# Softplus moved into attention, another product order in the MLPs' last quarter, and new orders of casts and scans

## The chip, the core and the metric

The kernel runs on one core of a Trainium2 chip. The metric is the device time of one execution in microseconds (us); of several runs the median is given. A core has five engines with queues of their own, which run each in order: TensorE (PE: matmuls and transposes), VectorE (DVE), ScalarE (ACT: activations, copies and casts), GpSimd (POOL) and SyncE (SP), which mainly issues DMA transfers. They wait for each other by semaphores.

## The reference, cut to what matters

Two layers over 512 tokens of width 1024, all in float32. Layer 0 mixes by stick-breaking attention with 16 heads, layer 1 by a gated linear recurrence (RG-LRU); each is followed by an MLP with squared ReLU.

```python
def stick_breaking_attention(h, w_qkv, w_o):      # per block of 128 queries
    z = einsum(q, k) * scale
    log_keep = where(mask, log_sigmoid(-z), 0)
    after = reversed_cumsum(log_keep) - log_keep
    w = where(mask, exp(log_sigmoid(z) + after), 0)
    return (w @ v) @ w_o

def rglru_block(h, w_in, ...):
    gate = gelu((h @ w_in)[..., :W])
    xc = causal_depthwise_conv((h @ w_in)[..., W:], conv_w, conv_b)     # 4 taps
    r = sigmoid(xc @ w_a + b_a);  i = sigmoid(xc @ w_x + b_x)           # 16 diagonal blocks
    log_a = -8 * r * softplus(-lam)
    a = exp(log_a);  b = sqrt(-expm1(2 * log_a)) * (i * xc)
    hs = associative_scan(a, b)                                         # h = a h + b
    return (hs * gate) @ w_o

def squared_relu_mlp(h, w1, w2):
    u = relu(h @ w1)
    return (u * u) @ w2

for layer in range(2):
    x = x + mixer(rms_norm(x, norm_mix[layer]))
    x = x + squared_relu_mlp(rms_norm(x, norm_mlp[layer]), w1, w2)
return rms_norm(x, norm_final)
```

## The kernel before

**Products.** Activations lie transposed, features on 128 partitions and 512 tokens in the free dimension, in eight chunks (`C` = 8). Every float32 product is done as three matmuls on operands split in two: a weight slab of 128x1024 is loaded by SP into `raw`, ScalarE casts it to `wh` (high part) and VectorE subtracts to give `wl` (low part) (`slab`, L184 and L191; for the MLP's second matrix `operand`, L834 and L835); the activations are split in the same way (`xgh`/`xgl` at L115 and L116, or `bh`/`bl`). `three` (L196 to L198) then issues high by high, high by low, low by high.

**Order.** The order on TensorE is the order in which the program emits its matmuls; a scheduler sets the order on the other engines, from the same emission order, and `tc.issue_after(i)` and `tc.high_priority()` bend it: with the first, what stands inside goes on its own engine behind instruction `i`. As each engine works its queue in order, a cast placed behind another instruction also waits for whatever that one waits for.

**Start.** The first slabs of q and k are loaded and cast in parts (`slab_parts`), x arrives in eight chunks, each cast by L115. `softplus` is a generator that computes `c4` and `c8` from the RG-LRU's lambda: absolute value, a sigmoid (L232), then 24 small VectorE operations on 128x8 tiles with a polynomial (L234 to L246). The first `yield` stands behind the sigmoid; its second piece is emitted in mid attention (`next(soft)`), its parts go where the scheduler finds place, which is from 8.6 us on. What it makes is first needed by `recur` in the RG-LRU. ScalarE's functions lie in tables; changing from one table to another appears in the trace as an ACT_TABLE_LOAD.

**Attention.** Eight pairs of heads. `score_steps(pair)` computes scores (L525, L526), two sigmoids on ScalarE (`w` at L533, `keep` at L534), a scan on VectorE (L542) and a product on GpSimd (L546). `value_steps(pair)` takes eight turns, one per head of the pair and block of keys: `turn` transposes the weights on TensorE (L564), ScalarE casts the head (`th`, L579), VectorE subtracts the tail (`tl`, L580), and `times` multiplies by the values (L590, L591). Between those steps `fill` puts matmuls that don't depend on them: projections of the next pair's q and k (`qk_steps`), of values (`v_steps`, L441 to L443), and, at the end, parts of the output product (`so_part`, `so_steps`, L196 to L198 on `bh`). Each `fill` step that starts a new weight begins with its `slab`: the DMA, the casts and the subtractions are emitted right there. Steps of scores and values are due at fixed counts of fill steps.

**MLP.** The second product of each MLP is done in four quarters (`q4`), each as seven block products P1 to P7 in place of eight (`PRODUCTS`); the weights' blocks are summed on VectorE (L854) or, for the names in `far`, by an accumulating DMA of GpSimd, then cast and cut (`operand`). A product has two groups `g`; `block` prepares its weight, `times` issues its matmuls (L866), `collect` adds its result to `c` (L875). In the last quarter the sums wait behind `self.ready`, the last split of activations (L815).

**RG-LRU.** For each of eight chunks: `conv` (projection, taps at L1058, cast to `bh`/`bl` at L1064 and L1065), `gates` (two gate products, L1078 to L1080, and sigmoids), `recur` (Tanh L1096, Exp L1098, Sqrt L1104 on ScalarE, the scan on VectorE), `gate` and `gated`. A list at the end of the stage gives their order.

**Tail.** `square` takes sums of squares of the finished rows (L1177), `finish` the bias (L1189), the root (L1190) and the scaling. For the last rows, two halves' sums are added first (L1225).

Of the kernel before, what the change touches and what calls it, by code (L numbers as in the profile page):

```python
# [47 lines left out]
def hybrid_encoder(  # L48
# [123 lines left out]
    adding, behind = [False], [None]  # L172

    def slab(src, cut=1, ks=range(C)):
# [7 lines left out]
        for i in range(cut):  # L182
            k = slice(ks.start + i * len(ks) // cut, ks.start + (i + 1) * len(ks) // cut)
            A.copy(wh[:, k, :], raw[:, k, :])  # L184
# [41 lines left out]
    def softplus():  # L226

        ab, pp, den, s1, s2, pl, _, _ = lams.values()
        lam = col("lam")
        V.tensor_scalar(ab, lam, -1.0, None, ALU.mult)  # L230
        V.tensor_tensor(ab, ab, lam, ALU.max)
        A.activation(pp, ab, AF.Sigmoid, scale=-1.0)  # L232
        yield
        V.tensor_scalar(den, pp, -1.0, 2.0, ALU.mult, ALU.add)  # L234
# [14 lines left out]
    soft = softplus()  # L249

# [12 lines left out]
    with ExitStack() as actx:  # L263
# [250 lines left out]
        late = {}  # L514
        turns = [0]

        def score_steps(pair):

            for j in range(2):
                for qb in range(NB):  # L520
# [13 lines left out]
                    A.activation(keep[:, :n], z[:, :n], AF.Sigmoid, scale=norm["rn"][:, qb : qb + 1])  # L534
# [21 lines left out]
        def value_steps(pair):  # L556
# [3 lines left out]
            def turn(j, kb):  # L560
# [17 lines left out]
                with tc.high_priority():  # L578
                    A.copy(dh, tr[:, :n])  # L579
                    left[j, kb] = V.tensor_tensor(dl, tr[:, :n], f(dh), ALU.subtract)  # L580

# [28 lines left out]
            for g in order[-2:]:  # L610
                times(*g)
                yield
            A.copy(bh[:, pair, :], o)
# [45 lines left out]
        for i in range(n_fill):  # L659
# [14 lines left out]
            if i == LATE // 2:  # L674

                next(soft)
# [42 lines left out]
    class Mlp:  # L719
# [109 lines left out]
        def operand(self, raw):  # L829
# [5 lines left out]
            V.tensor_tensor(wl, raw, f(wh), ALU.subtract)  # L835
            return wh, wl

        def block(self, q4, name, g, far):
# [11 lines left out]
            elif to:  # L850

                ahead = not far or (name, g) == ("P5", 0)
                with nullcontext() if ahead else tc.issue_after(self.ready.ins):
                    V.tensor_tensor(raw, raw, self.raws[to, g], ALU.add)  # L854
# [25 lines left out]
        def down(self, q4, far=(), end=None):  # L880
            sums = {}

            def product(name, g):
                w = self.block(q4, name, g, far)
# [6 lines left out]
                if g:  # L891
                    for i in range(2):
                        self.collect(name, i, sums[to][i])
# [7 lines left out]
            for g in range(2):  # L901
                for name in ("P1", "P5", "P2"):
                    product(name, g)
            for name in ("P6", "P3", "P7"):
                for g in range(2):
                    product(name, g)
            end([self.block(q4, "P4", g, far) for g in range(2)], sums["X"])
# [28 lines left out]
    with ExitStack() as mctx:  # L936
# [25 lines left out]
        def between(q4, c):  # L962
            if (q4, c) == (0, C - 1):
                next(soft)
# [27 lines left out]
    with ExitStack() as rctx:  # L992
# [29 lines left out]
        xc, aa, om, z, hs, gin, gw = ({} for _ in range(7))  # L1022
# [66 lines left out]
        def recur(chunks):  # L1089
            nonlocal mark  # L1090

            for c in chunks:
                a0 = rp2.tile([P, S], F32, tag="a0", name="a0")
                d = rp2.tile([P, S], F32, tag="d", name="d")
                with after(sig):
                    ex = A.activation(om[c], aa[c], AF.Tanh, scale=c4[:, c : c + 1])  # L1096
                with after(ex):
                    ex = A.activation(a0, aa[c], AF.Exp, scale=c8[:, c : c + 1])  # L1098
                V.scalar_tensor_tensor(d, a0, 1.0, om[c], ALU.add, ALU.mult)
                G.tensor_scalar(aa[c], d, -1.0, 1.0, ALU.mult, ALU.add)  # L1100
                V.scalar_tensor_tensor(xc[c], a0, 1.0, xc[c], ALU.add, ALU.mult)
            for c in chunks:
                with after(ex):
# [3 lines left out]
                with after(tap if c < 6 else None):  # L1107
# [18 lines left out]
        for what, c in (  # L1126
            (conv, 0), (conv, 1), (conv, 2), (gate, 0), (gate, 1), (gates, 0), (conv, 3), (gates, 1),
            (gate, 2), (gates, 2), (conv, 4), (gates, 3), (recur, range(3)), (conv, 5), (gates, 4),
            (gate, 3), (conv, 6), (gates, 5), (gate, 4), (conv, 7), (recur, range(3, 6)), (gates, 6),
            (gate, 5), (gated, range(6)), (gate, 6), (gates, 7), (recur, range(6, C)), (gate, 7),  # L1130
# [21 lines left out]
    with ExitStack() as mctx:  # L1152
# [22 lines left out]
        def square(t, h, i, cols=slice(0, S)):  # L1175
# [3 lines left out]
            )  # L1179

# [4 lines left out]
        def finish(t, h, i, cut=None):  # L1185
# [3 lines left out]
            V.tensor_scalar(bias[:, t : t + 1], ss[:, t, 0:1], 1.0 / D, EPS, ALU.mult, ALU.add)  # L1189
# [12 lines left out]
        def end(ws, xs):  # L1202
            for t in range(2):
                square(t, 0, 0)
                scaled(t, 0)
                square(t, 1, 1)
# [7 lines left out]
            square(2, 0, 1)  # L1214
# [80 lines left out]
```

## Time and profile before

| | |
|---|---|
| median of 3 runs | 1083.8 us (1083.19 to 1087.09) |
| profiled execution | 1083.88 us |
| its span, first to last instruction | 1081.9 us |
| mean granted TensorE clock | 0.996 |
| busy: PE, DVE, ACT, POOL | 1061.7, 823.7, 569.5, 171.3 us |
| HBM read, written | 104.91 MB, 2.10 MB |

The profile is of one execution. A row of its timeline gives the start in us from the span's start, the duration in us, engine, line and operation, the tile written and those read, the shape, and in brackets how long the engine was idle before it and whom it waited for. Successive matmuls overlap, so their distance in time is from start to start. The granted clock is the share of full speed that the throttle gave TensorE.

### The profile page before, as it was taken

The page shows a single profiled execution, that of the slowest core. Times are in us where ns is not written, and L with a number is a line of the kernel's source. Part 1 is how long each engine was busy: PE and PEld are TensorE (multiplying, and loading weights), DVE is VectorE, ACT ScalarE, POOL GpSimd, SP SyncE. Part 2 cuts the span into 40 slices and gives each one's busy share as a digit, 9 for nine tenths or more (in the row PEclk, how much of TensorE's full clock was granted, in tenths as well). Part 3 has the DMA queues.
Part 4 walks back from the last instruction along what each step waited for, and adds up shares of the span by engine and source line. Part 5 has one row for each costly group of instructions (what it writes and reads, how often), then busy time and mean ns, then how long its engine had stood idle before and what let it go on. Part 6 is the DMA issues. An engine that isn't in the chain of part 4 may idle for free.

```text
span 1081.9 us, 13604 instructions
## 1 busy us (share of the span) xinstructions
PE 1061.7 (98%) x4992; PEld 880.2 (81%) x4992; DVE 823.7 (76%) x1078; ACT 569.5 (53%) x823; POOL 171.3 (16%) x199
## 2 busy tenths in 40 slices
PE   8999999999999999999999999999999999999987
PEld 7888888888888888888878777887888888888876
DVE  7788787838796597597687769975686597597686
ACT  7667676726455344344345468853454344344344
POOL 2344344420000000000001564122000000000002
PEclk8999999999999999999999999999999999999999
DMA  6754454426305305305332695252305305305103
GB/s 211 200 137 137 100 157 105 140 96 235 105 9 186 117 3 192 117 1 185 100 84 61 166 217 140 78 175 98 98 23 191 98 20 181 111 20 177 57 13 104
DMA packets 44034, 125.71 MB, mean 116 GB/s; under 512 B 7744, under 2 KB 8512, under 8 KB 43968
## 3 DMA queue, kind: packets, MB, share of 16 engines
q1 hardware_dynamic: 41088, 115.94, 34.4%
q0 software_dynamic: 2304, 8.39, 4.5%
q8 instruction: 39, 0.64, 0.3%
q10 hardware_dynamic: 576, 0.52, 0.1%
q14 instruction: 27, 0.22, 0.1%
HBM read 104.91 MB, written 2.10 MB: 99 GB/s over the span
## 4 chain that ended last, share of the span: by engine, by line
PE 84%; DVE 6%; ACT 5%; DMA 3%; issue 1%; SPq 0%; ACTq 0%; DVEq 0%
PE ps_t L866 10%; PE ps_o L866 6%; PE ps_acc L196 6%; PE ps_acc L197 6%; PE ps_acc L198 6%; PE ps_z L866 6%; PE ps_acc L866 5%; PE ps_o L196 4%; PE ps_o L198 4%; PE ps_o L197 4%; PE ps_t L197 3%; PE ps_t L196 3%; PE ps_t L198 3%; PE ps_z L196 3%; PE ps_z L197 3%; PE ps_z L198 3%
## 5 line engine op out<-in xcount | busy, mean ns | idle before, releaser
L184 ACT CAST wh<-raw 128x1024 fp32r<-128x1024 f32 (+2 forms) x136 | 119.8, 901 | 132.7 <-PE ps_o L198 33.4
L834 ACT CAST wh<-b 128x1024 fp32r<-128x1024 f32 x96 | 100.6, 1051 | 134.1 <-PE ps_o L866 25.0
L191 DVE TENSOR_TENSOR wl<-raw,wh 128x1024 fp32r<-128x1024 f32 (+2 forms) x126 | 131.7, 1062 | 24.9 <-ACT wh L184 24.8
L835 DVE TENSOR_TENSOR wl<-b,wh 128x1024 fp32r<-128x1024 f32 x96 | 117.5, 1226 | 27.0 <-ACT wh L834 26.9
L196 PE MATMUL ps_acc<-xgh,wh 128*128 128x512 f32 x304 | 123.7, 407 | 2.1 <-ACT xgh L115 1.4
L197 PE MATMUL ps_acc<-xgh,wl 128*128 128x512 f32 x304 | 120.2, 395 | 0.3 <-DVE wl L166 0.3
L198 PE MATMUL ps_acc<-xgl,wh 128*128 128x512 f32 x304 | 119.9, 395 | 0.0
L849 POOL DMA_DIRECT2D b<-in_w_dn x6 | 5.4, 903 | 639.6 <-DVE wl L835 316.9
L542 DVE TENSOR_TENSOR_SCAN scan<-keep,later 128x128 f32<-128x128 f32 (+1 forms) x64 | 60.6, 948 | 18.7 <-ACT keep L534 10.3
L196 PE MATMUL ps_o<-xgh,wh 128*128 128x512 f32 x176 | 69.5, 395 | 0.2 <-DVE x L695 0.2
L197 PE MATMUL ps_o<-xgh,wl 128*128 128x512 f32 x176 | 68.6, 390 | 0.0
L198 PE MATMUL ps_o<-xgl,wh 128*128 128x512 f32 x176 | 68.6, 390 | 0.0
L198 PEld LDWEIGHTS ps_acc<-xgl,wh 128*128 128x128 f32 x304 | 57.7, 190 | 12.9 <-DVE xgl L116 0.3
L196 PEld LDWEIGHTS ps_acc<-xgh,wh 128*128 128x128 f32 x304 | 57.8, 190 | 12.8 <-ACT xgh L115 1.8
L788 ACT ACTIVATE u<-u 128x512 f32<-128x512 f32 x64 | 39.3, 629 | 52.5 <-DVE u L787 52.5
L196 PE MATMUL ps_t<-xgh,wh 128*128 128x512 f32 x168 | 66.5, 396 | 0.0
L197 PEld LDWEIGHTS ps_acc<-xgh,wl 128*128 128x128 f32 x304 | 58.0, 191 | 10.2 <-DVE wl L166 0.6
L197 PE MATMUL ps_t<-xgh,wl 128*128 128x512 f32 x168 | 65.7, 391 | 0.0
L198 PE MATMUL ps_t<-xgl,wh 128*128 128x512 f32 x168 | 65.5, 390 | 0.0
L546 POOL TENSOR_TENSOR w<-w,scan 128x128 f32<-128x128 f32 (+1 forms) x64 | 53.4, 836 | 52.4 <-DVE scan L542 49.7
L854 DVE TENSOR_TENSOR b<-b,b 128x1024 f32<-128x1024 f32 x46 | 55.7, 1219 | 0.2
L798 DVE TENSOR_TENSOR u<-u 128x256 f32<-128x256 f32 x128 | 49.5, 420 | 2.6 <-ACT u L788 1.9
(327 smaller groups left out, 2750.9 us busy)
## 6 DMA issues: line engine op xcount, KB each, us to landing
raw<-in_w_m SPq DMA_DIRECT2D x64, 512.0 KB, 3.5
b<-in_w_dn SPq DMA_DIRECT2D x48, 512.0 KB, 3.9
raw<-in_w_dn SPq DMA_DIRECT2D x16, 512.0 KB, 3.6
raw<-in_w_in SPq DMA_DIRECT2D x16, 512.0 KB, 4.3
raw<-in_w_qk SPq DMA_DIRECT2D x12, 512.0 KB, 3.5
wl<-raw POOLq DMA_DIRECT2D x10, 512.0 KB, 5.8
x<-in_xT SPq DMA_DIRECT2D x16, 256.0 KB, 4.3
raw<-in_w_ro SPq DMA_DIRECT2D x8, 512.0 KB, 3.4
```

What stands on the lines that cost most here:

```text
L184: A.copy(wh[:, k, :], raw[:, k, :])
L191: V.tensor_tensor(wl[:, k, :], raw[:, k, :], f(wh[:, k, :]), ALU.subtract)
L196: PE.matmul(ps, wh, ah, start=start, stop=False)
L197: PE.matmul(ps, wl, ah, start=False, stop=False)
L198: PE.matmul(ps, wh, al, start=False, stop=stop)
L542: V.tensor_tensor_scan(sc[:, S - n : S][:, ::-1], keep[:, :n][:, ::-1], later[:, S - n :][:, ::-1], 1.0, ALU.mult, ALU.max,)
L546: G.tensor_tensor(wt, wt, sc[:, S - n + 1 : S + 1], ALU.mult)
L798: V.tensor_tensor(u[:, out, :], u[:, x, :], u[:, y, :], op)
L834: A.copy(wh, raw)
L835: V.tensor_tensor(wl, raw, f(wh), ALU.subtract)
L854: V.tensor_tensor(raw, raw, self.raws[to, g], ALU.add)
L866: PE.matmul(ps, x[:, block, ts], y[:, jj, cols], start=first and n == 0, stop=last and n == 2, skip_group_check=not new,)
```

## The change

- **Softplus.** The generator now hands back control before anything is computed. In mid attention it is resumed with the latest `keep` activation, and the sigmoid is issued behind that; the 24 small operations are issued behind the split `mlp.ready` of the first MLP's first quarter.
- **Heads.** In pairs 0, 6 and 7 each turn records its head cast and its tail subtraction; every `slab` emitted until the pair's end casts behind that head and subtracts behind that tail.
- **Last quarter of each MLP.** The groups of the first three products are P1, P5, P2 and then P1, P2, P5 (before: P1, P5, P2 twice). Weights are prepared two products ahead of their matmuls. A sum of blocks (L854) is issued behind the cut of the block prepared before it, for P5's second group behind the last split, and P2's collects behind the newest cut.
- **RG-LRU.** `recur` is split in `rates` (Tanh, Exp and the factors) and `recur` (Sqrt and the scans); for chunks 0 to 2 the scans come after the sixth convolution, and the Tanh of chunks 0 to 2 behind the latest convolution's cast to `bh`.
- **Tail.** The bias is formed on ScalarE, right behind the squares, in place of a VectorE operation for each row block and an addition.

```diff
     slabs, loads = count(), count()
-    adding, behind = [False], [None]
+    adding, behind, heads = [False], [None], [None]
+    def behind_act():
+        return tc.issue_after(heads[0]) if heads[0] else nullcontext()
...
             k = slice(ks.start + i * len(ks) // cut, ks.start + (i + 1) * len(ks) // cut)
-            A.copy(wh[:, k, :], raw[:, k, :])
+            with behind_act():
+                A.copy(wh[:, k, :], raw[:, k, :])
             if adding[0]:
...
+        sigmoid = yield
         V.tensor_scalar(ab, lam, -1.0, None, ALU.mult)
         V.tensor_tensor(ab, ab, lam, ALU.max)
-        A.activation(pp, ab, AF.Sigmoid, scale=-1.0)
-        yield
-        V.tensor_scalar(den, pp, -1.0, 2.0, ALU.mult, ALU.add)
+        with tc.issue_after(sigmoid.ins):
+            A.activation(pp, ab, AF.Sigmoid, scale=-1.0)
+        with tc.issue_after((yield).ins):
+            V.tensor_scalar(den, pp, -1.0, 2.0, ALU.mult, ALU.add)
         V.reciprocal(den, den)
...
     soft = softplus()
+    next(soft)
...
-        late = {}
+        late, marks = {}, {}
         turns = [0]
...
                     A.activation(wt, z[:, :n], AF.Sigmoid, scale=norm["rp"][:, qb : qb + 1])
-                    A.activation(keep[:, :n], z[:, :n], AF.Sigmoid, scale=norm["rn"][:, qb : qb + 1])
+                    marks["keep"] = A.activation(
+                        keep[:, :n], z[:, :n], AF.Sigmoid, scale=norm["rn"][:, qb : qb + 1]
+                    )
                     t = wt[:, qb * P : n]
...
                 with tc.high_priority():
-                    A.copy(dh, tr[:, :n])
+                    head = A.copy(dh, tr[:, :n])
                     left[j, kb] = V.tensor_tensor(dl, tr[:, :n], f(dh), ALU.subtract)
+                if pair in (0, PAIRS - 2, PAIRS - 1):
+                    heads[0], behind[0] = head.ins, left[j, kb].ins
...
                 yield
+            heads[0] = behind[0] = None
             A.copy(bh[:, pair, :], o)
...
-
-                next(soft)
+                soft.send(marks["keep"])
             while done < len(due) and due[done][0] < i + 1:
...
             A.copy(wh, raw)
-            V.tensor_tensor(wl, raw, f(wh), ALU.subtract)
+            self.cut = V.tensor_tensor(wl, raw, f(wh), ALU.subtract)
             return wh, wl
...
-                ahead = not far or (name, g) == ("P5", 0)
-                with nullcontext() if ahead else tc.issue_after(self.ready.ins):
+                ahead = None
+                if far and (name, g) != ("P5", 0):
+                    ahead = self.ready if name == "P5" else self.before
+                with tc.issue_after(ahead.ins) if ahead else nullcontext():
                     V.tensor_tensor(raw, raw, self.raws[to, g], ALU.add)
...
-            def product(name, g):
-                w = self.block(q4, name, g, far)
+            def product(name, g, w=None):
+                w = w or self.block(q4, name, g, far)
                 to = self.PRODUCTS[name][3]
...
                 if g:
-                    for i in range(2):
-                        self.collect(name, i, sums[to][i])
+                    first = end and name == "P2"
+                    with tc.issue_after(self.cut.ins) if first else nullcontext():
+                        for i in range(2):
+                            self.collect(name, i, sums[to][i])
...
-            for g in range(2):
-                for name in ("P1", "P5", "P2"):
-                    product(name, g)
-            for name in ("P6", "P3", "P7"):
-                for g in range(2):
-                    product(name, g)
-            end([self.block(q4, "P4", g, far) for g in range(2)], sums["X"])
+            order = [("P1", 0), ("P5", 0), ("P2", 0), ("P1", 1), ("P2", 1), ("P5", 1)]
+            order += [(name, g) for name in ("P6", "P3", "P7", "P4") for g in range(2)]
+            ws = {}
+            def prepare(*at):
+                self.before = self.cut
+                ws[at] = self.block(q4, *at, far)
+            for at in order[:2]:
+                prepare(*at)
+            for at, ahead in zip(order[:-2], order[2:]):
+                prepare(*ahead)
+                product(*at, ws.pop(at))
+            end([ws["P4", g] for g in range(2)], sums["X"])
...
             if (q4, c) == (0, C - 1):
-                next(soft)
+                soft.send(mlp.ready)
...
-        xc, aa, om, z, hs, gin, gw = ({} for _ in range(7))
+        xc, aa, om, z, hs, gin, gw, a0s, exps = ({} for _ in range(9))
...
+        def rates(chunks):
+            for c in chunks:
+                a0 = rp2.tile([P, S], F32, tag="a0", name="a0")
+                with after(sig), after(high if c < 3 else None):
+                    ex = A.activation(om[c], aa[c], AF.Tanh, scale=c4[:, c : c + 1])
+                with after(ex):
+                    exps[c] = ex = A.activation(a0, aa[c], AF.Exp, scale=c8[:, c : c + 1])
+                a0s[c] = a0
+                if c != 2:
+                    factors(c)
+        def factors(c):
+            a0 = a0s[c]
+            d = rp2.tile([P, S], F32, tag="d", name="d")
+            V.scalar_tensor_tensor(d, a0, 1.0, om[c], ALU.add, ALU.mult)
+            G.tensor_scalar(aa[c], d, -1.0, 1.0, ALU.mult, ALU.add)
+            V.scalar_tensor_tensor(xc[c], a0, 1.0, xc[c], ALU.add, ALU.mult)
...
-
+            ex = exps[chunks[-1]]
             for c in chunks:
-                a0 = rp2.tile([P, S], F32, tag="a0", name="a0")
-                d = rp2.tile([P, S], F32, tag="d", name="d")
-                with after(sig):
-                    ex = A.activation(om[c], aa[c], AF.Tanh, scale=c4[:, c : c + 1])
-                with after(ex):
-                    ex = A.activation(a0, aa[c], AF.Exp, scale=c8[:, c : c + 1])
-                V.scalar_tensor_tensor(d, a0, 1.0, om[c], ALU.add, ALU.mult)
-                G.tensor_scalar(aa[c], d, -1.0, 1.0, ALU.mult, ALU.add)
-                V.scalar_tensor_tensor(xc[c], a0, 1.0, xc[c], ALU.add, ALU.mult)
-            for c in chunks:
+                if c == 2:
+                    with after(low):
+                        factors(c)
                 with after(ex):
...
-                with after(tap if c < 6 else None):
+                with after(low if c < 3 else tap if c < 6 else None):
                     V.tensor_tensor_scan(om[c], aa[c], xc[c], 0.0, ALU.mult, ALU.add)
...
             (conv, 0), (conv, 1), (conv, 2), (gate, 0), (gate, 1), (gates, 0), (conv, 3), (gates, 1),
-            (gate, 2), (gates, 2), (conv, 4), (gates, 3), (recur, range(3)), (conv, 5), (gates, 4),
-            (gate, 3), (conv, 6), (gates, 5), (gate, 4), (conv, 7), (recur, range(3, 6)), (gates, 6),
-            (gate, 5), (gated, range(6)), (gate, 6), (gates, 7), (recur, range(6, C)), (gate, 7),
+            (gate, 2), (gates, 2), (conv, 4), (gates, 3), (rates, range(3)), (conv, 5),
+            (recur, range(3)), (gates, 4), (gate, 3), (conv, 6), (gates, 5), (gate, 4), (conv, 7),
+            (rates, range(3, 6)), (recur, range(3, 6)), (gates, 6), (gate, 5), (gated, range(6)),
+            (gate, 6), (gates, 7), (rates, range(6, C)), (recur, range(6, C)), (gate, 7),
             (gated, range(6, C)),
...
-        def square(t, h, i, cols=slice(0, S)):
+        def square(t, h, i, cols=slice(0, S), end=False):
...
             )
+            if not end:
+                A.activation(
+                    bias[:, t : t + 1], ss[:, t, i : i + 1], AF.Identity,
+                    bias=bias[:, t : t + 1] if i else eps_t, scale=1.0 / D,
+                )
...
             rt = work.tile([P, 1], F32, tag="rt", name="rt")
-            V.tensor_scalar(bias[:, t : t + 1], ss[:, t, 0:1], 1.0 / D, EPS, ALU.mult, ALU.add)
             A.activation(rt, ss[:, t, i : i + 1], AF.Sqrt, bias=bias[:, t : t + 1], scale=1.0 / D)
...
                 scaled(t, 0)
-                square(t, 1, 1)
+                square(t, 1, 1, end=True)
                 finish(t, 1, 1)
...
             mlp.collect("P4", 0, xs[0])
-            square(2, 0, 1)
+            square(2, 0, 1, end=True)
             finish(2, 0, 1)
...
                 mlp.collect("P4", 1, ps, cols)
-                square(3, 0, 1 + i, cols)
+                square(3, 0, 1 + i, cols, end=i == 1)
                 if i == 0:
-                    V.tensor_tensor(ss[:, 3, 0:1], ss[:, 3, 0:1], ss[:, 3, 1:2], ALU.add)
                     scaled(3, 0, cols)
```

## The prediction

> **What bounds the kernel now.** I read the page's head and its chain of waits first, then the waits of TensorE by cause, then the start stretch by stretch of the granted clock, then the timeline around every gap of TensorE.
>
> ```profile
> span 1081.9 us, 13604 instructions
> ...
> PE 1061.7 (98%) x4992; PEld 880.2 (81%) x4992; DVE 823.7 (76%) x1078; ACT 569.5 (53%) x823; POOL 171.3 (16%) x199
> ...
> PE 84%; DVE 6%; ACT 5%; DMA 3%; issue 1%; SPq 0%; ACTq 0%; DVEq 0%
> ```
>
> TensorE is busy 98% of the span and 84% of the chain lies on it. The change leaves its matmuls alone but for the places of twelve of them. So only the remaining gaps can be won, and a new gap costs its full length.
>
> ```profile
> PE ps_acc L866 <- DVE wl L835: 3.4, 2, 2.9
> PE ps_t L564 <- DVE tl L580: 2.5, 3, 1.5
> PE ps_z L1080 <- DVE bl L1065: 1.5, 2, 1.1
> PE ps_z L1078 <- ACT bh L1064: 1.4, 1, 1.4
> PE ps_acc L196 <- ACT xgh L115: 1.4, 1, 1.4
> ```
>
> Columns: total us, times, longest. These five causes hold 10.2 us: the last quarter of an MLP, the turns of attention, the RG-LRU's convolutions, and the start. The change aims at all of them, and adds waits of its own in attention. A second reserve is the clock:
>
> ```profile
> 5.15:8.56 3.41, 1.61 (x6) 0.66 (x5) 1.73 (x5) 3.35 (x7) 0.00 (x0) 1.00 0.92 291
> 8.56:11.97 3.41, 2.75 (x7) 2.08 (x8) 3.14 (x11) 3.41 (x8) 0.00 (x0) 0.50 0.97 343
> 11.97:15.39 3.42, 3.42 (x10) 2.64 (x9) 3.38 (x8) 3.42 (x7) 1.33 (x1) 0.50 0.52 200
> ```
>
> Columns: length, busy us of PE, PEld, DVE, ACT and POOL, then the granted clock. TensorE was busy 47% (1.61 of 3.41) of one stretch, and the clock was 0.50 for the next two; from 15.39 us on it is full.
>
> **The change part by part** (negative is a gain).
>
> *A. Softplus leaves the start.*
>
> ```profile
> 7.05 1.28 ACT L232 ACT_TABLE_LOAD   x1
> 9.22 0.79 PE L196 MATMUL ps_acc<-xgh,wh 128*128 128x512 f32 x1 [1.41 <-ACT xgh L115]
> 10.67 0.63 PE L196 MATMUL ps_acc<-xgh,wh 128*128 128x512 f32 x1
> 11.09 0.63 PE L197 MATMUL ps_acc<-xgh,wl 128*128 128x512 f32 x1
> 15.62 0.39 PE L196 MATMUL ps_acc<-xgh,wh 128*128 128x512 f32 x1
> 15.85 0.39 PE L197 MATMUL ps_acc<-xgh,wl 128*128 128x512 f32 x1
> ```
>
> The table load ahead of ScalarE's sigmoid sits before the second cast of x, and TensorE waits 1.41 us for it. In the changed program the sigmoid comes after attention's, with their table; the load goes, and the matmul can start at 9.22 - 1.41 = 7.81. What that is worth depends on the clock, since a matmul starts every 0.42 us at half clock and every 0.23 at full. Before, 15.39 - 9.22 = 6.2 us at half clock pass some 14.4 matmuls. From 7.81, full clock until 8.56 passes 0.75/0.23 = 3.3. Three courses follow. If both halves stay: 3.3 + 6.83/0.42 = 19.5 matmuls by 15.39, 5.1 more than before, a gain of 5.1 x 0.23 = 1.2 us; less if casts lag, 0.9 as the near end. If the clock returns at 11.97, because the stretch before is now filled without a hole (2.75 of 3.41 before): 3.3 + 8.1 are done by then, the other 3.0 take 0.7, so the place is reached at 12.7 and the gain is 2.7. If it never drops: 14.4 x 0.23 = 3.3, reached at 11.1, a gain of 4.3. I take the middle course, less 0.2 for casts and loads that then arrive barely in time: **-2.5, between -0.9 and -4.3**. The first stretch would be busy (1.61 + 0.75)/3.41 = 69%, which lies between 47% and full and so settles nothing.
>
> The Trainium skill ("TensorE: Matmul & The Clock Gate", Part 1: The HAM clock gate) says that a free-running window of 4096 cycles, some 3.4 us, is judged as a whole, that an idle one halves the clock and that one busy window restores it. The stretches here are 3.41 us long, which agrees; but a window that was 81% busy did not restore the clock at once, and by the rule alone the sum would take the course of 2.7.
>
> The 24 small operations behind the sigmoid go to the first down phase of the first MLP.
>
> ```profile
> L240 DVE TENSOR_TENSOR pl<-pl,s x7: 158/164/1258, 12.2 to 26.6; 128x8 f32<-128x8 f32 x7
> 311.00:335.00 24.00, 24.00 (x106) 19.44 (x105) 18.94 (x21) 13.75 (x17) 0.00 (x0) 1.00 0.30 102
> ```
>
> At 0.16 us each (the middle of the first row) they need 3.9 us; VectorE has 24.00 - 18.94 = 5.06 us to spare in those 24 us, and TensorE is full there. Nothing, then, with 0 to +1 if one stands ahead of a weight's subtraction at the wrong moment.
>
> *B. Orders in attention's first half.* The raw slab that held up the casts comes later now, so this gap's 0.24 and the pipe refill behind it go: **-0.4** (0 to -0.4).
>
> ```profile
> 42.79 0.38 PE L525 MATMUL ps_z<-kh,q 128*128 128x256 f32 x1 [0.24 <-DVE keep L531]
> ```
>
> *C. Pair 0: a slab's casts now stand behind the latest turn's head copy, its subtractions behind the turn's tail.* The good of it: the 1.5 us (longest wait for tl above) of the transposes goes. The price: where a slab's first matmul follows a turn directly, its cast can't be ready.
>
> ```profile
> 67.40 0.38 PE L564 MATMUL ps_t<-ident,w 128*128 128x128 f32 x2
> 67.54 0.36 PE L441 MATMUL ps_acc<-wh,xgh 128*128 128x256 f32 x1
> 67.74 0.28 PE L442 MATMUL ps_acc<-wl,xgh 128*128 128x256 f32 x1
> ...
> 67.85 1.14 ACT L184 CAST wh<-raw 128x512 fp32r<-128x512 f32 x2
> 68.89 0.48 ACT L533 ACTIVATE w<-ps_z,rp 128x256 f32<-128x256 f32 x1
> 69.25 0.48 ACT L534 ACTIVATE keep<-ps_z,rn 128x256 f32<-128x256 f32 x1
> 69.61 0.38 ACT L579 CAST th<-ps_t 128x256 fp32r<-128x256 f32 x1
> ...
> 68.63 1.28 DVE L191 TENSOR_TENSOR wl<-raw,wh 128x512 fp32r<-128x512 f32 x2
> ```
>
> The values' slabs of the second group are first used at 67.54, 0.14 us after the transposes. Today they were cast long before. In the changed order ScalarE runs from 67.85, where the two casts stand today, the two activations (0.36 from start to start), then this head, then eight slab casts. The head starts at 67.85 + 0.72 = 68.57 and ends at 68.95; half a slab (1.14/2) is ready at 69.5: TensorE waits 2.0 us. VectorE's half subtraction (1.28/2) comes at 70.15, against a matmul that wants it 0.2 after its forerunner: +0.5. The second pair's q slab, first used just behind the third turn, waits by the same sum (half a cast, then its subtraction behind two tails) +0.5 and +1.2. Together 4.2 less 1.5 gained: **+2.7, between 0**, if the waits let later work catch up, **and +5**. The upper end counts what stands behind: eight casts of 0.57 hold ScalarE for 4.6 us, ahead of the next scores' activations, and the slabs' raw buffers come free later, so the third pair's loads do too.
>
> *D, E. Pairs 6 and 7, the same order.*
>
> ```profile
> 201.92 0.47 PE L196 MATMUL ps_acc<-bh,wh 128*128 128x512 f32 x1
> 208.56 0.63 PE L564 MATMUL ps_t<-ident,w 128*128 128x128 f32 x4 [0.70 <-DVE tl L580]
> 209.26 0.40 PE L196 MATMUL ps_acc<-bh,wh 128*128 128x512 f32 x1
> ...
> 226.57 0.38 PE L564 MATMUL ps_t<-ident,w 128*128 128x128 f32 x2
> 226.71 0.48 PE L196 MATMUL ps_z<-bh,wh 128*128 128x512 f32 x1
> ...
> 227.04 0.37 ACT L579 CAST th<-ps_t 128x256 fp32r<-128x256 f32 x1 [1.19 <-PE ps_t L564]
> ```
>
> In pair 7 the output product's slab is wanted at 226.71, and its cast now follows the head that ends at 227.41; half a slab takes 0.57, so 227.98: +1.25, then +0.35 for the subtraction; I take +1.4 (0 to +2.5). In pair 6 two slabs (at 201.92 and 209.26) have the same sequence, +1.3 and +0.5 each, and a third only the late subtraction, some +1.2: +4.8. The waits there now, the other two for tl (2.5 - 1.5 = 1.0) with refills some 2.0, go: +2.8, taken as **+2.5** (-2 to +5).
>
> *F. MLP 0, last quarter.*
>
> ```profile
> 559.30 0.50 PE L866 MATMUL ps_acc<-wl,sh 128*128 128x512 f32 x1 [0.51 <-DVE wl L835]
> ```
>
> Blocks are prepared two products ahead and the third product's collects stand behind the newest cut, so this subtraction comes in time: -0.7 with the refill. The next product's cut then has one collect more before it: +0.35. **-0.35** (-0.7 to +0.3).
>
> *G. RG-LRU.* The convolution's cast to bh leaves its place behind Tanh and Exp; both waits (1.4 and 1.1 of the rows above, 2.8 with refills) go. But the seventh block of gates now stands earlier than its operands:
>
> ```profile
> 674.62 1.05 ACT L184 CAST wh<-raw 128x1024 fp32r<-128x1024 f32 x1
> 676.75 0.39 PE L1078 MATMUL ps_z<-bh,gh 128*128 128x512 f32 x1
> ```
>
> A slab's cast of 1.05 goes ahead of the bh cast, which is ready at about 675.5 against an arrival some 2 to 3 us before 676.75: +1.8. **-1.0** (-2.8 to 0).
>
> *H. MLP 1, last quarter.*
>
> ```profile
> 1041.41 4.62 DVE L854 TENSOR_TENSOR b<-b,b 128x1024 f32<-128x1024 f32 x4
> 1047.82 0.50 PE L866 MATMUL ps_acc<-wl,sh 128*128 128x512 f32 x1 [2.88 <-DVE wl L835]
> ```
>
> Four sums of blocks in a row hold VectorE while TensorE waits for a cut behind them. Each sum now goes behind the cut of the block before: the 2.9 and its refill, 3.0, go; the last of the group's cuts is late by about half of one (1.2/2): **-2.5** (-3.0 to -1.9).
>
> *I. The tail.*
>
> ```profile
> 1075.14 0.68 DVE L1225 TENSOR_TENSOR ss<-ss 128x1 f32<-128x1 f32 x1
> ```
>
> This addition stands before the last collect and goes; ScalarE forms the bias earlier, in idle time: **-0.55** (-0.7 to -0.3).
>
> Sum: -2.5 - 0.4 + 2.7 + 2.5 + 1.4 - 0.35 - 1.0 - 2.5 - 0.55 = -0.7. The profiled execution took 1083.88 us, so 1083.2; the median of the three runs shown is 1083.8, 0.1 lower, so **1083 us**.
>
> **The rivals.** *The head order costs no more than the gaps that it closes* (C, D and E together 0, since PE's order leaves the matmuls the time that I deny them): for it speaks that the same waits for tl recur in every one of these pairs; against it the 0.14 us between the turn at 67.40 and the slab. The sum is then -7.3: 1076.5 us. Chance 0.32.
>
> *The slabs become the bound of attention*, the slower side: C, D and E at their upper ends, +12.5, because the pile of casts on ScalarE also delays scores and loads, with the clock as before (-0.9). Sum: 12.5 - 0.9 - 0.4 - 4.4 = +6.8, 1090.6 us. It decides from about 11 us of waits for slabs on. For it: eight casts in a row at one place; against: ScalarE is busy 53% only and can catch up. Chance 0.20.
>
> *The clock decides alone.* If it does not drop at all, the sum falls by 1.8 to 1081; if it stays halved as long as before, it rises by 1.6 to 1085. Both lie inside the forecast's bound and are counted there. That the change does not do what it says would show as the table load still at 7 us; the changed program no longer has it.
>
> **How the numbers follow.** About 0.5% (5.4 us) is what a measurement of this kernel can tell from no change. My forecast, 1083 with a range of its own of 1079 to 1088, has 0.48 and counts as no change; faster has 0.32, slower 0.20. The range that should hold 8 in 10 reaches from a little below the faster case (1074.5: that case with the clock never dropping) to just short of the slower one (1089.5).
>
> **What would show it.** Right: no table load at 7 us and the second x cast directly behind; the granted clock back by 12 us; the 2.9 at 1047.8 gone, with a wait under 1 us a product later; new waits of L441 for wh near 67 us and of L196 for wh L184 near 202, 209 and 227. Wrong: no wait for wh of L184 in attention above 0.5 us (then the faster case), waits for it that sum to more than 11 us (the slower), the clock at half from 8.6 to 15.4 as before, or a wait at the end of the softplus chain near 320 us.

## The result and the profile after

The changed kernel takes **1100.84 us** (median of 4 runs, 1098.21 to 1102.68) against 1083.72: ratio 1.0149, 95% interval 1.0117 to 1.0182, so 1.5% slower. The prediction said 1083, no change, with 0.20 for slower. The profiled execution took 1099.24 us with a span of 1097.4, 15.5 more than before.

Head of the profile of the changed kernel, and its waits of TensorE by cause (total us, times, longest):

```profile
span 1097.4 us, 13596 instructions
...
PE 1069.1 (97%) x4992; PEld 885.6 (81%) x4992; DVE 819.9 (75%) x1073; ACT 569.1 (52%) x826; POOL 164.3 (15%) x199
```

```profile
PE ps_acc L201 <- DVE wl L195: 4.1, 4, 1.6
PE ps_z L1104 <- ACT bh L1090: 3.6, 1, 3.6
PE ps_acc L200 <- ACT wh L188: 3.6, 4, 1.4
PE ps_z L533 <- DVE keep L539: 1.7, 1, 1.7
PE ps_acc L449 <- ACT wh L188: 1.7, 1, 1.7
...
PE ps_z L200 <- ACT wh L188: 1.1, 1, 1.1
PE ps_acc L450 <- DVE wl L195: 1.0, 1, 1.0
```

Of the five causes of before, those at the start and in the last quarter are gone or short, and the others have given way to new ones. L188 and L195 are a slab's cast and subtraction: their rows here sum to 11.5 us of waits for slabs in attention, where before there was none of note. L1104 is the RG-LRU's gates. And TensorE is busy 7.4 us *more* with the same 4992 matmuls: part of them ran slower. The clock by its windows shows where (the changed kernel; length, busy us of PE, PEld, DVE, ACT, POOL, then the granted clock; each row one window of 3.41 us):

```profile
54.90:58.31 3.41, 1.66 (x6) 0.82 (x5) 2.94 (x5) 2.21 (x6) 0.93 (x2) 1.00 0.02 4
58.31:61.72 3.41, 3.41 (x10) 2.75 (x10) 1.71 (x3) 1.21 (x3) 0.29 (x1) 0.50 0.93 205
61.72:65.14 3.42, 3.42 (x20) 2.91 (x20) 1.05 (x3) 1.77 (x3) 1.16 (x2) 1.00 0.91 251
68.55:71.96 3.41, 0.85 (x5) 0.66 (x6) 3.27 (x6) 3.41 (x9) 0.93 (x2) 1.00 0.55 122
71.96:75.38 3.42, 3.42 (x16) 3.23 (x15) 2.49 (x5) 0.72 (x2) 0.00 (x0) 0.50 0.89 216
208.50:211.91 3.41, 1.72 (x7) 1.28 (x8) 1.93 (x3) 1.28 (x4) 0.64 (x1) 1.00 0.09 23
211.91:215.32 3.41, 3.41 (x10) 2.66 (x9) 0.96 (x1) 1.11 (x3) 1.16 (x2) 0.50 0.36 131
225.57:228.98 3.41, 1.98 (x8) 1.05 (x6) 2.44 (x5) 3.38 (x8) 1.07 (x2) 1.00 0.11 37
228.98:232.39 3.41, 2.42 (x12) 2.03 (x13) 3.41 (x5) 1.79 (x4) 1.05 (x2) 1.00 0.79 250
689.77:693.19 3.42, 0.90 (x3) 0.46 (x4) 3.42 (x6) 3.41 (x6) 1.94 (x1) 1.00 0.47 149
693.19:696.60 3.41, 3.41 (x9) 2.65 (x10) 3.38 (x5) 2.05 (x3) 1.46 (x1) 0.50 0.04 12
```

Four times a window in which TensorE was busy 25 to 50% is followed by one at half clock, which then passes half the matmuls (x10 against x20). A window of 58% (1.98 of 3.41) is followed by one at full clock. By the matmuls' distances the four half windows after new waits cost 1.5, 1.5, 1.3 and 1.6 us, together 5.9. The slab waits ahead of the first three sum to 1.8, 2.7 and 1.8 us, so in attention the clock adds more than half of the waits' own length again. The four runs agree in this: 1098.21 and 1099.24 us had a mean clock of 0.993, 1102.43 and 1102.68 had 0.989 and 0.987.

Because the matmuls keep their order, but for two groups of twelve that change places in the last quarter of each MLP, the matmul at the same place can be followed in both traces; the difference of its start times, stage by stage, is the account of the change:

| step | predicted | measured | the matmul's start, before and after |
|---|---|---|---|
| A start | -2.5 | -3.0 | 15.36, 12.33 |
| B first orders | -0.4 | +1.5 | 42.79, 41.29 |
| C pair 0 | +2.7 (0 to 5) | +7.2 | 74.13, 79.87 |
| between pairs 0 and 6 | 0 | +0.7 | 120.99, 127.42 |
| D pair 6 | +2.5 (-2 to 5) | +6.7 | 216.82, 229.97 |
| E pair 7 | +1.4 (0 to 2.5) | +1.8 | 227.03, 242.01 |
| F MLP 0 | -0.35 | -0.5 | 559.30, 573.77 |
| G RG-LRU | -1.0 (-2.8 to 0) | +2.9 | 679.08, 696.49 |
| H MLP 1 | -2.5 | -2.5 | 1056.12, 1071.04 |
| H, a collect near the end | in H | +1.0 | 1070.62, 1086.55 |
| I tail | -0.55 | -0.4 | the span's end |

The sum of the third column is 15.4.

### The profile page after: what moved, and what is told of

Same layout as the page of the kernel before. It is cut to its first block, busy times and chain, and to the rows that moved or that the text cites. A ratio compares the mean times of both kernels' runs of the same rounds, so it can differ in the third digit from the quotient of the medians.

```text
span 1097.4 us, 13596 instructions
## 1 busy us (share of the span) xinstructions
PE 1069.1 (97%) x4992; PEld 885.6 (81%) x4992; DVE 819.9 (75%) x1073; ACT 569.1 (52%) x826; POOL 164.3 (15%) x199
## 4 chain that ended last, share of the span: by engine, by line
PE 84%; DVE 7%; ACT 4%; DMA 3%; issue 2%; SPq 0%; DVEq 0%; ACTq 0%
PE ps_t L881 9%; PE ps_o L881 6%; PE ps_acc L201 6%; PE ps_acc L202 6%; PE ps_acc L200 6%; PE ps_z L881 6%; PE ps_acc L881 5%; PE ps_o L200 4%; PE ps_o L202 4%; PE ps_o L201 4%; PE ps_t L201 3%; PE ps_t L200 3%; PE ps_t L202 3%; PE ps_z L201 3%; PE ps_z L202 3%; PE ps_z L200 3%
## 5 line engine op out<-in xcount | busy, mean ns | idle before, releaser
L188 ACT CAST wh<-raw 128x1024 fp32r<-128x1024 f32 (+2 forms) x136 | 119.4, 902 | 131.3 <-PE ps_o L202 35.3
L195 DVE TENSOR_TENSOR wl<-raw,wh 128x1024 fp32r<-128x1024 f32 (+2 forms) x126 | 130.7, 1056 | 23.5 <-ACT wh L188 23.3
L552 DVE TENSOR_TENSOR_SCAN scan<-keep,later 128x128 f32<-128x128 f32 (+1 forms) x64 | 57.8, 904 | 30.8 <-ACT keep L542 20.2
L200 PEld LDWEIGHTS ps_acc<-xgh,wh 128*128 128x128 f32 x304 | 58.3, 192 | 11.5 <-ACT wh L188 0.8
L556 POOL TENSOR_TENSOR w<-w,scan 128x128 f32<-128x128 f32 (+1 forms) x64 | 50.7, 793 | 64.8 <-DVE scan L552 62.1
```

The source lines that it names most:

```text
L195: V.tensor_tensor(wl[:, k, :], raw[:, k, :], f(wh[:, k, :]), ALU.subtract)
L200: PE.matmul(ps, wh, ah, start=start, stop=False)
L552: V.tensor_tensor_scan(sc[:, S - n : S][:, ::-1], keep[:, :n][:, ::-1], later[:, S - n :][:, ::-1], 1.0, ALU.mult, ALU.max,)
L556: G.tensor_tensor(wt, wt, sc[:, S - n + 1 : S + 1], ALU.mult)
```

## The experiments

### Is it the order behind the turns?

The order taken out of the changed kernel, and put alone into the kernel before:

```diff
-                if pair in (0, PAIRS - 2, PAIRS - 1):
-                    heads[0], behind[0] = head.ins, left[j, kb].ins
```

> The changed kernel, but no slab's cast or subtraction is ordered behind a turn. Theory W (the order of casts makes new waits in attention, and long waits make the clock drop): of the 15.7 us that pairs 0, 6 and 7 lost in the changed kernel nearly all comes back, less the 3.6 us of gaps that the kernel before had there and less nothing for the start: time 1084 to 1088, no stretch at half clock before 300 us. Rival S (attention only shows what the earlier start and the moved sigmoid disturb, through later transfers): the waits for wh and wl of slabs stay within a third, time above 1094.

> The kernel before with the order of casts and subtractions alone. Theory W: slower by 13 to 17 us, 1097 to 1101, with the waits of the changed kernel near 58, 67, 202, 209, 217 and 227 us and half clock behind the longest. Rival S: within 4 us of before.

Measured: without the order 1082.22 us against 1085.34 for the kernel before beside it, ratio 0.9973 (0.9960 to 0.9987); the order alone 1103.98, ratio 1.0163 (1.0132 to 1.0194). Theory W stands, Rival S falls: this one edit, by itself, costs as much as the whole change (1.0149, 1.0117 to 1.0182). Both times lie outside the ranges expected, by 1.8 and 3.0 us, each on the side of a dearer order. In the trace of the run without it no window before 300 us is at half clock, no wait for a slab's cast or subtraction in attention is left, and the longest waits are these:

```profile
PE ps_z L1101 <- ACT bh L1087: 3.6, 1, 3.6
PE ps_t L574 <- DVE tl L590: 3.6, 4, 1.5
```

The second row is the gap that the order was to close (2.5 us in the kernel before), the first is the RG-LRU's new wait, which is there with and without it.

### Which half of it, the casts or the subtractions?

```diff
-                    heads[0], behind[0] = head.ins, left[j, kb].ins
+                    behind[0] = left[j, kb].ins     # the other run: heads[0] = head.ins
```

> The changed kernel, but only the subtractions stand behind a turn's tail, the casts where the scheduler puts them. If the casts' order is the costly half: the waits for wh go (4.7 us in attention and the waits for wl that follow from a late cast), 1086 to 1090. If the subtractions' order is as bad: waits for wl of 1 to 2 us remain at the same places, 1092 to 1098.

> The changed kernel, but only the casts stand behind a turn's head, the subtractions where the scheduler puts them. With the subtractions alone ordered the time was as with both. If each of the two orders holds the second matmul of a slab by itself (theory B): 1094 to 1102 here as well, with waits for wh of 1 to 2 us in attention and shorter ones for wl. If the subtractions' order alone is to blame: below 1088.

Measured: subtractions alone 1104.08 us, ratio 1.0169 (1.0155 to 1.0183); casts alone 1101.01, ratio 1.0148 (1.0126 to 1.0170). Either half costs as much as both, against my expectation for the subtractions, which had put most of the price on the casts. With the subtractions alone ordered, the values' slab shows why. First TensorE, then VectorE and ScalarE:

```profile
66.07 0.36 PE L449 MATMUL ps_acc<-wh,xgh 128*128 128x256 f32 x1
70.16 0.46 PE L450 MATMUL ps_acc<-wl,xgh 128*128 128x256 f32 x1 [3.73 <-DVE wl L195]
...
68.69 0.40 DVE L590 TENSOR_TENSOR tl<-ps_t,th 128x256 fp32r<-128x256 f32 x1
69.01 4.11 DVE L195 TENSOR_TENSOR wl<-raw,wh 128x512 fp32r<-128x512 f32 x6
...
66.02 0.61 ACT L188 CAST wh<-raw 128x512 fp32r<-128x512 f32 x1
```

The casts are done in time and the first matmul starts without a wait, but the second needs `wl`, and all the slabs' subtractions stand behind the tail at 68.69. TensorE waits 3.73 us at one matmul where in the changed kernel it waited 1.74 for `wh` and 0.97 for `wl`. The subtraction also depends on the cast, so ordering the casts alone makes both late: the values' slab then waits 1.74 us for `wh` and 0.96 for `wl`, as with both orders. The two waits don't add; they take each other's place.

### Does the clock drop because of the waits?

Matmuls whose results are thrown away, into the same bank ahead of the first real one, fill two of the waits:

```diff
+                for _ in range(22 if (m, t) == (1, 0) else 0):       # values, second group
+                    PE.matmul(ps, xgh[:, 0, ts], xgh[:, 1, : 2 * P], start=True, stop=True)
+            for _ in range(8 if (i, pair) == (0, 2) else 0):         # q of the third pair
+                PE.matmul(ps, xgh[:, 0, :P], xgh[:, 1, :], start=True, stop=True)
```

> The changed kernel with its order of casts, and matmuls whose results are thrown away ahead of two slabs' first matmuls: 8 of 128x512 (8 x 0.23 = 1.8 us) before the third pair's q, 22 of 128x256 (22 x 0.12 = 2.6 us) before the second group's values. They add work where TensorE waited 1.75 and 2.7 us. If the half clock follows from a stretch with too little work (theory C): no half clock between 55 and 77 us, the extra matmuls cost nothing, 2 to 3.5 us faster than the changed kernel there. If the clock drops for another reason, as at a fixed place of the program: half clock as before at 58 and 72 us, and the time is the same or up to 2 us more.

Measured: 1100.44 us, ratio 1.0132 (1.0107 to 1.0156), which does not part from the changed kernel's 1.0149. The trace does. Rows 55 to 77 us of this run, then of the changed kernel:

```profile
55.00:77.00 22.00, 21.45 (x131) 18.77 (x129) 16.35 (x27) 14.21 (x32) 5.95 (x13) 1.00 0.52 131
```

```profile
55.00:77.00 22.00, 17.55 (x83) 14.58 (x82) 14.49 (x23) 12.94 (x29) 5.55 (x11) 0.84 0.57 144
```

From the last matmul before the q slab to the end of pair 0's slabs TensorE takes 21.1 us with 30 matmuls more, against 24.5 without them (57.82 to 78.90, and 55.40 to 79.87): 3.4 us less, and no half window. Theory C stands at this place: the waits cost the clock. The run with free factors (next section) shows the same without any filler: its pair 0 has the same four waits (0.33, 1.42, 1.74 and 0.96 us), but the clock's windows fall on them at another phase, only one half window follows (at 70.37), and the pair costs 5.8 us in place of 7.2. The run's total gains nothing, since other stretches fell to half clock in its profile (from 43.8 and from 286 us).

### What turns the RG-LRU's gain into a loss?

```diff
-                if c != 2:
-                    factors(c)
+                factors(c)
...
-                if c == 2:
-                    with after(low):
-                        factors(c)
```

> The changed kernel, but the factors of the third chunk are not held behind the sixth convolution's tail. Theory F (ScalarE's root waits 4.2 us for these held factors, and all that it does until the seventh convolution's cast is late by that): the wait of 3.6 us before the seventh gates goes or falls below 1 us, with the half clock behind it: 4 to 6 us faster than the changed kernel, 1095 to 1097. Rival R (the three gaps closed earlier only bring TensorE sooner to a cast that ScalarE's tables bound): the wait stays above 2.5 us and the time within 1.5 us of the changed kernel.

Measured: 1095.5 us, ratio 1.0087 (1.0061 to 1.0114). In the changed kernel ScalarE and VectorE stood thus:

```profile
677.03 0.63 ACT L1142 ACTIVATE om<-om 128x512 f32<-128x512 f32 x1 [4.20 <-DVE d L1130]
...
676.34 0.66 DVE L1130 SCALAR_TENSOR_TENSOR d<-a,om 128x512 f32<-128x512 f32 x1
...
690.89 0.60 ACT L1090 CAST bh<-bt 128x512 fp32r<-128x512 f32 x1
691.55 0.50 PE L1104 MATMUL ps_z<-bh,gh 128*128 128x512 f32 x1 [3.59 <-ACT bh L1090]
```

The root (L1142) is held 4.2 us by `d`, which waits in VectorE's queue behind the sixth convolution's tail, and ScalarE works its queue in order. With free factors the wait of 3.59 and the half clock behind it are gone: Theory F stands. But another wait has come:

```profile
PE ps_o L1106 <- DVE bl L1091: 2.5, 2, 2.1
```

Through the RG-LRU this trace loses 1.2 us against the kernel before (offset 12.94 to 14.14), where the changed kernel lost 2.9. So the edit is worth 1.7 of the 3.2 us by which the two profiled spans differ; the other 1.5 lie ahead of it, most of them in pair 0, where this trace has one half window and the changed kernel two. The medians are 5 us apart, so they are no measure of this edit alone.

The same without the order behind the turns, and two ways to go on from it:

> The changed kernel without the order behind the turns and with the third chunk's factors free. If the two costs add up: 18 us for the first and 4 to 5 for the second, 1077 to 1079, clearly below the kernel before. If TensorE, arriving earlier in the RG-LRU, meets the next late cast there: 1080 to 1082.

> Without the order behind the turns, third chunk's factors free, and the scans of chunks 3 to 5 behind the eighth convolution's tail in place of its last tap. Theory Q (the wait of 2.1 us of the last gates for their low part comes from three scans, 3.45 us, queued ahead of that subtraction on VectorE): the wait falls below 0.5 us, 1.5 to 2.5 us faster than the run with free factors alone (1081.0), so 1078.5 to 1079.5, if what waits for these scans has slack. If it has none, a wait of the same size appears at the output product some 10 us later, and the time is the same.

> The changed kernel without the order behind the turns and with the RG-LRU stage as in the kernel before. If the new order of that stage is a loss as a whole even with free factors (1.3 us by the traces): 1 to 1.5 us faster than the run with free factors (1081.0), so 1079.5 to 1080. If it is a gain: 1081.5 or more.

```diff
-                with after(low if c < 3 else tap if c < 6 else None):
+                with after(low if c < 6 else None):
                     V.tensor_tensor_scan(om[c], aa[c], xc[c], 0.0, ALU.mult, ALU.add)
```

Measured: free factors 1081.04 us (0.9955, 0.9943 to 0.9967); scans moved as well 1081.13 (0.9964, 0.9951 to 0.9977); the whole stage as before 1080.36 (0.9956, 0.9941 to 0.9970). So the two costs don't add up to 1077 to 1079; the other expectation, 1080 to 1082, holds. The intervals overlap, and the runs alone don't rank the three; the traces tell what happens. With free factors, VectorE and then TensorE:

```profile
683.67 3.45 DVE L1139 TENSOR_TENSOR_SCAN om<-aa,bt 128x512 f32<-128x512 f32 x3
...
687.62 0.68 DVE L1088 TENSOR_TENSOR bl<-bt,bh 128x512 fp32r<-128x512 f32 x1
...
688.35 0.50 PE L1103 MATMUL ps_o<-bl,gh 128*128 128x512 f32 x1 [2.10 <-DVE bl L1088]
```

With the scans behind the subtraction that wait is gone, and this one, of the same size, stands 7 us later at the output product:

```profile
695.55 0.50 PE L200 MATMUL ps_o<-bh,wh 128*128 128x512 f32 x1 [2.23 <-ACT aa L1108]
```

So Theory Q is right on the cause, and its second branch on the worth. VectorE is busy 37.7 of the 40 us from 660 on in the run with free factors, and a gap closed in this stage opens again downstream. With the stage as before its two old gaps are back (1.4 and 1.1), and from there to 680 us the trace loses nothing but one half window (1.2 us in the end).

### The parts that work

> The kernel before with softplus moved alone. If the start's gain lasts: 3 us faster, 1081. If it is given back where the second pair's stacked q lands (the wait for keep at 41 us that grew by 1.5 us in the changed kernel) and at the sigmoid in mid attention (0.7): 1.0 us faster or less, 1082.5 to 1084.

> The kernel before with the new order of the MLPs' last quarters alone. By the traces of the changed kernel: -0.5 in the first MLP, -2.95 at the last quarter's gap of the second, +0.5 and +0.9 at its later cuts and collects, so 2 us faster than before. If those gains hang on the rest of the change: within 1 us of before.

Measured: softplus moved, alone: 1082.86 us, ratio 0.9977 (0.9959 to 0.9994). The new last quarters, alone: 1081.9 us, ratio 0.9970 (0.9958 to 0.9983), some 3 us, one more than the 2 expected. Its trace bears out the 2: -0.8 and +0.4 in the first MLP, -3.1 at the second's gap, +0.7 and +0.8 behind; the other 1.2 us of its shorter span lie in the start, which this edit doesn't touch. Softplus's time fits the second branch of its expectation, but not for the reason given there: the wait for `keep` at 41 us didn't come. Its trace gains 2.65 us up to 45 us; 0.3 is given back at 205 us, 0.6 at the first MLP's norm, which VectorE finishes late, and 1.0 by a half window at 649.6.

### A wait at the end

> As the run without that order and with free factors, and besides the last product's weights are prepared where they were before, behind the seventh product's collects. Theory P (the wait of 0.6 us for VectorE near the end comes from three cuts queued ahead of a collect, because those weights are prepared earlier): that wait goes, 0.5 to 1 us faster than the run without this edit. Otherwise the same within 0.3 us.

```diff
-                prepare(*ahead)
+                if ahead[0] != "P4":
+                    prepare(*ahead)
...
-            end([ws["P4", g] for g in range(2)], sums["X"])
+            end([self.block(q4, "P4", g, far) for g in range(2)], sums["X"])
```

Measured: 1080.68 us, ratio 0.9948 (0.9935 to 0.9962), against 1081.04 (0.9955) without it: the same. The wait is still there, and so are the three cuts in a row ahead of the collect:

```profile
1062.59 4.59 DVE L845 TENSOR_TENSOR wl<-b,wh 128x1024 fp32r<-128x1024 f32 x3
...
1067.18 0.67 DVE L887 TENSOR_TENSOR c<-c,ps_t 128x512 f32<-128x512 f32 x1
```

Theory P's place of emission is not what sets that order; what does stays open.

## Why the prediction failed, step by step

**Attention's order (C, D, E): the mechanism was right, the size was not.** Predicted were +6.6 us, measured +15.7: 9.1 of the 16.1 us missed, and beyond the upper ends of C and D. The single waits came out nearly as worked out: for the values' slab 2.0 and 0.5 were forecast, 1.74 and 0.97 measured, for q 0.5 and 1.2 against 0.33 and 1.42. The step that failed is that these waits were priced at their own length. The prediction read, in its first part, that a stretch 47% busy is followed by half clock, and applied it to the start alone; the waits that it forecast in attention leave windows of 25 to 50%. That is 4.3 of the 9.1 us missing (1.5, 1.5 and 1.3). Most of the rest is pair 6, taken at +2.5: the third slab's waits came to 2.4 us where 1.2 was forecast (1.63 for its subtraction, and 0.78 for its cast, which was not forecast), and its six waits moved the matmuls by some 1.3 us more than their own length, the refill of the pipe, which the prediction counted only for the gaps that go.

**The slower rival had the right place.** It put the pile of casts at the end and the bound at 11 us of waits; the waits for slabs sum to 11.5. Its price of 12.5 lacked the clock: without the three half windows C, D and E measured 11.4. Of the delay of scores that it asked for, one wait shows, the 1.75 us of B below.

**RG-LRU (G): a wrong sign.** The two old waits went, as forecast (-1.6 and -1.3 at these matmuls). The step that failed is the wait before the seventh gates, priced at 1.8: it came to 3.8 with the pipe refill, 0.9 more at the next operand and 1.6 of half clock. Not seen was that the third chunk's factors, moved behind the sixth convolution, hold ScalarE's root for 4.2 us.

**Start (A): the size came, by luck.** The middle course was full clock until 8.56 us, half until 11.97, then full. The trace shows another: half clock from the first product on, until 10.5 us, then full, with no drop between. Rows of the changed kernel:

```profile
6.06 0.80 PE L200 MATMUL ps_acc<-xgh,wh 128*128 128x512 f32 x1 [0.32 <-ACT wh L165]
...
7.91 0.63 PE L200 MATMUL ps_acc<-xgh,wh 128*128 128x512 f32 x1
8.34 0.63 PE L201 MATMUL ps_acc<-xgh,wl 128*128 128x512 f32 x1
...
10.47 0.42 PE L200 MATMUL ps_acc<-xgh,wh 128*128 128x512 f32 x1
10.73 0.40 PE L201 MATMUL ps_acc<-xgh,wl 128*128 128x512 f32 x1
10.96 0.39 PE L202 MATMUL ps_acc<-xgl,wh 128*128 128x512 f32 x1
```

The first takes 0.80 us, like the one at half clock in the kernel before (9.22, 0.79), and up to 10.47 they stand 0.43 apart, then 0.23. (The granted clock of the profile reads 1.00 in this stretch; the matmuls' distances say that it was not.) In the run without the order behind the turns the start's edit is the same, the clock is full from 5.3 us on, with no half window in the start, and the matmul of A's row stands at 11.20, 4.2 us earlier than before: the course called "never drops". So what A is worth changes with where the windows fall.

**First orders (B): taken as a gain of 0.4, it gave back half of A.** VectorE's `keep` for the next scores (L539) stands behind `xl` (L316), which needs ScalarE's cast `xh` (L315), and that waits for the transfers that stack q. First the changed kernel, then the run without the order behind the turns:

```profile
38.68 0.62 ACT L315 CAST xh<-ks 128x512 fp32r<-128x512 f32 x1 [3.59 <-DMA q<-xh]
39.94 0.69 DVE L316 TENSOR_TENSOR xl<-ks,xh 128x512 fp32r<-128x512 f32 x1 [4.90 <-ACT keep L542]
40.55 0.69 DVE L539 TENSOR_TENSOR keep<-ps_z,r 128x512 f32<-128x512 f32 x1
41.29 0.39 PE L533 MATMUL ps_z<-kh,q 128*128 128x256 f32 x1 [1.75 <-DVE keep L539]
```

```profile
38.33 0.67 DVE L539 TENSOR_TENSOR keep<-ps_z,r 128x512 f32<-128x512 f32 x1
39.05 0.62 ACT L315 CAST xh<-ks 128x512 fp32r<-128x512 f32 x1 [1.18 <-DMA q<-xh]
39.26 0.28 PE L533 MATMUL ps_z<-kh,q 128*128 128x256 f32 x1
40.19 0.69 DVE L316 TENSOR_TENSOR xl<-ks,xh 128x512 fp32r<-128x512 f32 x1 [1.19 <-ACT keep L542]
```

The transfers are no quicker there, but `keep` stands ahead of `xl`, and TensorE doesn't wait. This matmul waits 1.1 to 3.7 us in the six profiles with an order behind the turns, of casts, subtractions or both, and not at all in the seven changed ones without; in six of these the next scores, 2.5 us later, wait 0.4 to 0.7 us, once 1.6. So most of B's loss is one more price of that order, beside the 15.7 us. Why the scheduler then puts `keep` behind `xl` stays open. With softplus moved alone the matmul gains the 0.4 that was forecast.

**Between pairs 0 and 6.** The 0.7 us are two waits for tails, at 111.2 and 127.4 us, both ahead of the moved sigmoid, which runs at 134.45; the run with softplus alone passes both places without a loss. So the sigmoid is not their cause; what is stays open.

**Last quarters and tail (F, H, I).** F and the gap of H came as forecast (-0.5 and -2.5), and the run with them alone confirms it. Not forecast was the wait for a collect behind three cuts near the end, +1.0 with its refill; the run with the last quarters alone has it too, so it belongs to H and takes a good part of its gain. I came as forecast: -0.4 against -0.55.

## What to carry to other kernels

A cast that is ordered behind another instruction inherits all that this one waits for; where its consumer on the bounding engine follows that instruction directly, the order makes a wait of the whole latency, and the gaps that it closed elsewhere did not pay for it here. Price a wait on TensorE together with the clock: where it left a window half empty or more, the next window ran at half speed in four cases of six here. The parts of this change that pay are the softplus and the last quarters; with the RG-LRU stage as before and no order behind the turns it took 1080.36 us, 0.44% under the kernel before (0.9956, 0.9941 to 0.9970).

## What the hardware showed unexpectedly

The drop of the clock after windows that were only half idle. Of the changed kernel's windows above, those with TensorE busy 25, 26, 49 and 50% (0.85, 0.90, 1.66 and 1.72 us) were followed by half clock, those of 58 and 71% were not. The line isn't sharp: two more windows of the same execution, with 50 and 47%, kept the full clock:

```profile
37.83:41.25 3.42, 1.71 (x15) 1.51 (x13) 1.31 (x3) 1.50 (x3) 0.00 (x0) 1.00 0.87 226
686.36:689.77 3.41, 1.60 (x7) 0.94 (x5) 3.41 (x7) 3.39 (x5) 1.98 (x2) 1.00 0.01 5
```

Over the 14 profiles, by the granted clock and the busy time of each window, the windows at full clock with TensorE busy at most 46% were all followed by half clock (20 of 20), those with 47 to 53% mostly (16 of 19), those with 55 to 59% once in 11; above that it happened once, after 74%.

The windows keep one phase through an execution (58.31, 71.96, 211.91 and 693.19 us lie whole windows apart), and another in the next. So the same waits may cost the clock or not, as pair 0 with one half window or two shows. The kernel before has one of 2.88 us near its end that falls over two windows, busy 63 and 53%, and the clock stays:

```profile
1042.80:1046.21 3.41, 2.14 (x10) 1.45 (x8) 3.41 (x4) 2.87 (x3) 0.00 (x0) 1.00 0.00 0
1046.21:1049.62 3.41, 1.80 (x8) 1.50 (x9) 3.41 (x5) 0.00 (x0) 0.00 (x0) 1.00 0.00 0
```

The Trainium skill ("TensorE: Matmul & The Clock Gate", Part 1: The HAM clock gate) says that the window runs free and that an idle one halves the clock. The phase agrees; but here a window half busy was mostly enough.
